# Encoder layer on one core: the first MLP product by Strassen's scheme, all hidden activations made first

## The chip, the core and the metric

The kernel runs on one core of a Trainium2 chip. The metric is the device time of one execution, in microseconds (us); lower is better. TensorE (PE) multiplies matrices, with its weight loads (PEld) listed apart; VectorE (DVE), ScalarE (ACT) and GpSimd (POOL) do elementwise work; SyncE (SP) and ScalarE issue the transfers (DMA) from and to DRAM. Matmul results land in PSUM banks; everything else lies in SBUF.

## What is computed

One encoder layer on 768 tokens (512 of a prompt, 256 of a sample), float32, width 1024. Mixer and cross attention come first; the change is in the MLP at the end:

```python
def _layer(x, ...):
    ...
    x = x + _rms_norm(_cross_attention(h, mem, xa_wq, xa_wkv, xa_wo, mem_g), g_post_xa)
    h = _rms_norm(x, g_pre_mlp)
    x = x + _rms_norm(jnp.square(jax.nn.relu(h @ w1)) @ w2, g_post_mlp)   # w1: 1024 x 4096, w2: 4096 x 1024
    return x
```

## The kernel before

**Three matmuls for one.** Every float32 operand is cut into a high part, rounded by a copy on ACT, and a low part, the rest, by a subtraction on DVE. A product is then three matmuls: high by high, high by low, low by high (`mm3`, L188 to L190; L1195 to L1197 in `up`). Activations are cut by `split` (L183 on ACT, L184 on DVE); weights by the class `Weights` (L108 on ACT, L109 on DVE), in units of 128x1024 elements. `W.get(key, ahead)` returns a unit and first emits the cutting of `ahead` further units in the order of the plan (`plan_c`). The high and low tiles of the units lie in groups of three in two slots; a slot comes free when all three units of its group have been used.

**Order.** The kernel is written in the Tile framework: the program order gives priorities, and the framework lays out each engine's queue before the run, by its own estimate of when operands and buffers are ready. On the chip each queue then runs in that order.

**The MLP.** The hidden width of 4096 is cut into eight blocks of 512. `up` makes one quarter (128 hidden features) of a block per weight unit: 8 steps of depth, three matmuls each, for the sample (256 columns) and for the prompt (512 columns), so 48 matmuls for a unit. ACT then applies relu (L1199) and POOL squares (L1200). `down` multiplies the block by its rows of `w2` by Strassen's scheme: the block's output, 768 tokens by 1024, is a 2x2 matrix product of halves of 384 tokens, 256 hidden features and 512 outputs, done with seven products instead of eight. A product is 18 matmuls of 512 columns (three groups of six). The sums and differences that the scheme needs are made on POOL: four per block of activations (L1218, 128x768) and four per block of weight quadrants (L997, 128x1024, in `quadrants`). Results are added into 18 accumulators (`acc`, six sets of three tiles of 128x512) by DVE from PSUM (L1239; in block 0 the first touch of a set is a copy on ACT, L1237). That is 24 additions per block, since product 1 goes into two sets.

**Sequence.** `STRASSEN` (L25) sets the order by hand: the seven products of block b are interleaved with the four quarters of `up` for block b + 1. Block 0's `up` stands before (the sample's part in the tail of the attention, L265, the prompt's at L1206). Block 7 is not in the scheme: `down_last` does it plainly, with 144 matmuls, combines the accumulators on POOL (L1257) and finishes the tiles (`finish`).

**Buffers.** Two high and two low tiles hold the cut activations of a product (`hh`, `hl`, `bufs=2`), and PSUM has four banks `mm` (for `up`) and four `y` (for `down`).

Of the kernel before, what the change touches and what calls it, by code (L numbers as in the profile page):

```python
# [6 lines left out]
F32 = mybir.dt.float32  # L7
F32R = mybir.dt.float32r
AF = mybir.ActivationFunctionType
ALU = mybir.AluOpType  # L10
# [14 lines left out]
STRASSEN = (("p", 1), ("up", 0), ("p", 2), ("p", 6), ("up", 1), ("p", 7), ("up", 2), ("p", 4), ("p", 5), ("up", 3), ("p", 3))  # L25
# [56 lines left out]
class Weights:  # L82
# [3 lines left out]
    def __init__(self, nc, new, raw, lo):  # L86
        self.nc, self.new, self.raw = nc, new, raw
        self.sub = lambda key: lo(key).tensor_tensor
        self.q, self.done, self.n = [], {}, 0
# [4 lines left out]
    def emit(self, upto):  # L94
        while self.n < min(upto, len(self.q)):
# [21 lines left out]
class Kernel:  # L117
# [75 lines left out]
    def run(self):  # L193
# [55 lines left out]
        self.hT = {}  # L249

        def h_tiles(s0, nt, side):
            pool, g = self.open(f"hx{s0}", side=side)
            self.hT[s0] = tuple(pool.tile([P, 8, nt * P], F32R, name=f"hx{s0}{n}") for n in "hl")
            return g

        g_h4 = h_tiles(*SEQS[1], "right")
# [3 lines left out]
        g_h0 = h_tiles(*SEQS[0], "left")  # L260
# [3 lines left out]
        first = self.hidden(up)  # L264
        self.up(0, 4, first, "up", 0)  # L265
# [3 lines left out]
        wp, g_w = self.open("wD", side="right")  # L269
        self.W.raw, self.w2pool = (wp, 1024, 2), wp  # L270
        pool, g = self.open("mlp", side="left")
        self.mlp(pool, up, first)
        for x in (g, g_up, g_h0, g_w, g_h4, g_ps, g_big, g_dram, g_const):
            self.close(x)
# [61 lines left out]
    def scratch(self):  # L336
# [7 lines left out]
        self.d_x1 = d.tile([NT, P, D], F32, name="d_x1")  # L344
        self.d_x2 = d.tile([NT, P, D], F32, name="d_x2")
# [614 lines left out]
    def plan_c(self):  # L960
# [14 lines left out]
        p1 = lambda b, m: w.plan(("w1", b, m), w1[:, :, b * 512 + m * P:b * 512 + (m + 1) * P], 8, P)  # L975

        for m in range(4):
            p1(0, m)
        for b in range(7):
            quad = dict(self.quadrants(w2[:, 4 * b:4 * b + 4]))  # L980
            for x, i in STRASSEN:
                if x == "up":
                    p1(b + 1, i)
                else:
                    w.plan(("w2", b, i), quad[i], 2, 512)
# [4 lines left out]
    def quadrants(self, w2):  # L990
# [3 lines left out]
        new = lambda: self.w2pool.tile([P, 2, 512], F32, tag="quad", bufs=5, name="quad")  # L994
# [5 lines left out]
        def p1():  # L1000
            for i in range(2):
                for j in range(2):
                    B[i, j] = new()
                    nc.sync.dma_start(B[i, j], w2[:, 2 * i:2 * i + 2, 512 * j:512 * j + 512])
# [176 lines left out]
    def hidden(self, pool):  # L1181

# [140 lines left out]
```

## Time and profile before

| | |
|---|---|
| median of 3 runs | 1213.06 us (1211.43 to 1223.36) |
| the profiled execution's own time | 1215.08 us |
| its span in the trace | 1213.3 us, 17783 instructions |
| mean granted TensorE clock over the span | 0.963 of full speed |
| PE busy | 1120.0 us (92%), 6800 matmuls |
| DVE busy | 708.1 us (58%) |
| ACT busy | 529.4 us (44%) |
| POOL busy | 355.5 us (29%) |

How to read it: the span is the trace's first to last instruction; the 1.8 us that the execution's own time has beyond it lie around it. Busy shares are means over the layer's stages. The MLP fills the span from about 713 us on, so shares of the MLP alone are read from windows of the trace. A busy PE is not a PE at its peak, so its pace is read from the starts of successive matmuls.

### The profile page before, as it was taken

Reading aid. Unit: us, or ns where it says so; the run is one execution under the profiler, and the core shown is the slowest. Engines: PE = TensorE matmul, PEld = TensorE weight load, DVE = VectorE, ACT = ScalarE, POOL = GpSimd, SP = SyncE. Lnnn points to the kernel's source line nnn. Section 1 sums busy time; section 2 is a strip of 40 time slices with the busy share of each in tenths; the row PEclk is TensorE's granted clock in tenths of the full one; section 3 lists DMA queues with packets and bytes.
Section 4 is the critical chain, followed back from the end, with each engine's and each line's share of the span. In section 5 each row is a group of like instructions: output and inputs, shape, how many; then the busy total and the mean of one; then the engine's idle time right before and its main releaser. Section 6 shows DMA issues by size and latency. Waiting matters only on the chain.

```text
span 1213.3 us, 17783 instructions
## 1 busy us (share of the span) xinstructions
PE 1120.0 (92%) x6800; PEld 958.7 (79%) x6800; DVE 708.1 (58%) x1263; ACT 529.4 (44%) x1119; POOL 355.5 (29%) x415
## 2 busy tenths in 40 slices
PE   6998999976959998899899989999999999999995
PEld 5887888865857887678787778888888888888884
DVE  5313455799789452455535646365658565658656
ACT  5336767755474333433434534443233332333322
POOL 5353210011111020011100136353536353526461
PEclk9999999988989698899899999999999999999998
DMA  6355311211312028732622233122212222212114
GB/s 199 98 180 160 94 53 37 78 35 36 75 48 92 28 93 253 239 122 82 231 70 70 88 122 96 43 75 65 88 53 76 63 70 70 87 52 61 44 57 169
DMA packets 108703, 113.81 MB, mean 94 GB/s; under 512 B 10079, under 2 KB 81867, under 8 KB 108619
## 3 DMA queue, kind: packets, MB, share of 16 engines
q1 hardware_dynamic: 100971, 99.55, 27.3%
q10 hardware_dynamic: 7648, 13.13, 2.9%
q8 instruction: 53, 0.87, 0.3%
q14 instruction: 31, 0.25, 0.1%
HBM read 91.27 MB, written 21.39 MB: 93 GB/s over the span
## 4 chain that ended last, share of the span: by engine, by line
PE 42%; issue 3%; POOL 2%; DVE 2%; DMA 1%; ACT 1%; POOLq 0%; DVEq 0%; ACTq 0%
PE up L1195 7%; PE up L1196 7%; PE up L1197 7%; PE y L189 5%; PE y L188 5%; PE y L190 5%; POOL y L1257 1%; DMA raw<-in_xa_wo 1%; PE xa L1156 1%; PE xa L1137 1%; PE mm L1121 1%; PE mm L1120 1%; PE mm L1119 1%; POOL rs L153 1%; PE mm L188 0%
## 5 line engine op out<-in xcount | busy, mean ns | idle before, releaser
L1200 POOL TENSOR_TENSOR hid<-hid 128x256 f32<-128x256 f32 (+1 forms) x64 | 61.1, 955 | 220.3 <-ACT hid L1199 220.3
L190 PE MATMUL y<-w,hl 128*128 128x512 f32 x318 | 123.8, 389 | 0.5 <-DVE hl L184 0.5
L189 PE MATMUL y<-w,hh 128*128 128x512 f32 x318 | 123.7, 389 | 0.0
L188 PE MATMUL y<-w,hh 128*128 128x512 f32 x318 | 123.7, 389 | 0.0
L1239 DVE TENSOR_TENSOR y<-y,y 128x512 f32<-128x512 f32 x72 | 48.9, 683 | 106.8 <-PE y L190 106.8
L1199 ACT ACTIVATE hid<-up 128x256 f32<-128x256 f32 (+1 forms) x64 | 31.2, 488 | 174.3 <-PE up L1197 174.3
L1195 PE MATMUL up<-hx0h,w 128*128 128x512 f32 x256 | 100.0, 390 | 1.0 <-DVE hx0l L184 1.0
L1196 PE MATMUL up<-hx0l,w 128*128 128x512 f32 x256 | 99.9, 390 | 0.0
L1197 PE MATMUL up<-hx0h,w 128*128 128x512 f32 x256 | 99.6, 389 | 0.0
L109 DVE TENSOR_TENSOR w<-raw,w 128x1024 fp32r<-128x1024 f32 (+1 forms) x58 | 78.8, 1365 | 31.4 <-ACT w L108 31.4
L997 POOL TENSOR_TENSOR quad<-quad 128x1024 f32<-128x1024 f32 x28 | 77.7, 2774 | 33.8 <-DVE w L109 20.2
L109 DVE TENSOR_TENSOR w<-quad,w 128x1024 fp32r<-128x1024 f32 x49 | 73.2, 1505 | 11.9 <-ACT w L108 11.9
L1195 PE MATMUL up<-hx4h,w 128*128 128x256 f32 x256 | 72.2, 282 | 4.2 <-ACT hid L1199 4.2
L1196 PE MATMUL up<-hx4l,w 128*128 128x256 f32 x256 | 71.7, 280 | 0.1
L1197 PE MATMUL up<-hx4h,w 128*128 128x256 f32 x256 | 71.4, 279 | 0.0
L108 ACT ACTIVATE w<-raw 128x1024 fp32r<-128x1024 f32 (+1 forms) x58 | 55.3, 963 | 35.7 <-DMA raw<-in_w_out 11.0
L190 PEld LDWEIGHTS y<-w,hl 128*128 128x128 f32 x318 | 59.7, 188 | 13.3 <-DVE hl L184 0.9
L189 PEld LDWEIGHTS y<-w,hh 128*128 128x128 f32 x318 | 59.7, 188 | 12.4
L188 PEld LDWEIGHTS y<-w,hh 128*128 128x128 f32 x318 | 59.7, 188 | 12.4
L183 ACT ACTIVATE hh<-hid 128x768 fp32r<-128x768 f32 x37 | 31.4, 848 | 83.2 <-PE y L189 64.0
L184 DVE TENSOR_TENSOR hl<-hid,hh 128x768 fp32r<-128x768 f32 x37 | 43.0, 1162 | 24.8 <-ACT hh L183 24.6
L1195 PEld LDWEIGHTS up<-hx0h,w 128*128 128x128 f32 x256 | 48.1, 188 | 10.4 <-DVE hx0l L184 1.2
(373 smaller groups left out, 3114.5 us busy)
## 6 DMA issues: line engine op xcount, KB each, us to landing
raw<-in_mlp_w SPq DMA_DIRECT2D x36, 512.0 KB, 4.5
quad<-in_mlp_w SPq DMA_DIRECT2D x28, 512.0 KB, 4.6
raw<-in_w_in SPq DMA_DIRECT2D x44, 256.0 KB, 3.0
d_x<-x ACTq DMA_DIRECT2D x12, 512.0 KB, 2.6
x<-d_x SPq DMA_DIRECT2D x12, 512.0 KB, 3.7
x<-in_x_prompt SPq DMA_DIRECT2D x8, 512.0 KB, 4.0
raw<-in_xa_wkv SPq DMA_DIRECT2D x16, 256.0 KB, 3.2
d_att<-parts SPq DMA_DIRECT2D x12, 256.0 KB, 2.0
```

Source lines behind the costliest of these rows:

```text
L108: self.nc.scalar.activation(hi[:, c], raw, AF.Copy)
L109: self.sub(key)(out=lo[:, c], in0=raw, in1=hi[:, c].bitcast(F32), op=ALU.subtract)
L184: nc.vector.tensor_tensor(out=lo, in0=src, in1=hi.bitcast(F32), op=ALU.subtract)
L188: nc.tensor.matmul(ps, lh, rh, start=first, stop=False)
L189: nc.tensor.matmul(ps, lh, rl, start=False, stop=False)
L190: nc.tensor.matmul(ps, ll, rh, start=False, stop=last)
L997: nc.gpsimd.tensor_tensor(out=out, in0=x, in1=y, op=ALU.subtract)
L1195: nc.tensor.matmul(ps, wh[:, k], hh[:, k], start=k == 0, stop=False)
L1196: nc.tensor.matmul(ps, wh[:, k], hl[:, k], start=False, stop=False)
L1197: nc.tensor.matmul(ps, wl[:, k], hh[:, k], start=False, stop=k == 7)
L1200: nc.gpsimd.tensor_tensor(out=r, in0=r, in1=r, op=ALU.mult)
L1239: nc.vector.tensor_tensor(out=y, in0=y, in1=ps, op=ALU.add)
```

## The change

Blocks 1 to 7 of the first product are done by Strassen's scheme too, and the two products of the MLP no longer alternate.

- **Sums of the activations.** `first_layer` makes the four sums of halves of the normed activations that the scheme needs (S1 to S4, each a high and a low tile of 128x4x384) once, in three column pieces, on DVE, POOL and ACT, before the prompt's part of block 0.
- **First layer.** For each of the blocks 1 to 7, seven products (`up`): a product is two quarters, each 4 steps of depth by three matmuls of 384 columns, so 24 matmuls. The results are combined from PSUM on DVE (and one copy per quarter on ACT) in the one hidden tile R, ACT does relu and square, and ACT's queue writes the quadrant to a new DRAM tensor `d_r`. R has one buffer.
- **Weight quadrants of w1.** `quadrants` now serves both products: four differences on POOL for each block of `w1` as well.
- **Second layer.** The hidden blocks are read back from `d_r`. `down` takes block 0 alone and then the pairs (1, 2), (3, 4), (5, 6): for each Strassen product both blocks' matmuls accumulate in the same PSUM group of twelve, so the additions into `acc` come once per pair. The cut activations have three buffers instead of two; quadrants of odd blocks have a pool of their own. PSUM groups use `mm` and `y` in turn.
- **Limits.** `W.limit` keeps the cutting of units from running ahead into a stage whose pool is not open yet.
- Squaring of blocks 1 to 7 moves from POOL to ACT.

```diff
-STRASSEN = (("p", 1), ("up", 0), ("p", 2), ("p", 6), ("up", 1), ("p", 7), ("up", 2), ("p", 4), ("p", 5), ("up", 3), ("p", 3))
+STRASSEN = (1, 2, 6, 7, 4, 5, 3)
+BLOCKS = ((0,), (1, 2), (3, 4), (5, 6))
...
-        first = self.hidden(up)
-        self.up(0, 4, first, "up", 0)
+        first = up.tile([P, 4, TOK], F32, tag="R", bufs=1, name="hid")
+        self.up_first(4, first, "up", 0)
...
+        self.W.limit = self.n_first + 7
+        pool, g = self.open("st", side="right")
+        self.first_layer(pool, up, first)
+        for x in (g, g_h):
+            self.close(x)
+        self.W.limit = None
+        pool, g = self.open("mlp", side="right")
+        self.w2more = pool
+        self.second_layer(pool, up, first)
...
+        for b in range(1, 8):
+            quad_b = q1(b)
+            for i in STRASSEN:
+                w.plan(("w1", b, i), quad_b[i], 4, 256)
+        self.n_first = len(w.q)
+        for bs in BLOCKS:
+            quad = [q2(b) for b in bs]
+            for i in STRASSEN:
+                for b, q in zip(bs, quad):
+                    w.plan(("w2", b, i), q[i], 2, 512)
...
+    def up(self, b, p, R, left, tags=("mm", "y"), ahead=3):
...
+        at = lambda j, i: R[:, 2 * j:2 * j + 2, 384 * i:384 * i + 384]
+        u, v, c = at(1, 0), at(1, 1), at(0, 1)
+        wh, wl = self.W.get(("w1", b, p), ahead)
+        for m in range(2):
+            ps = self.ps(tags[m], "up")[:, :384]
+            f = slice(m * P, (m + 1) * P)
+            for k in range(4):
+                nc.tensor.matmul(ps, wh[:, k, f], hh[:, k], start=k == 0, stop=False)
+                nc.tensor.matmul(ps, wh[:, k, f], hl[:, k], start=False, stop=False)
+                nc.tensor.matmul(ps, wl[:, k, f], hh[:, k], start=False, stop=k == 3)
+            if p == 1:
+                nc.scalar.activation(u[:, m], ps, AF.Copy)
+                continue
+            for out, x in {2: ((at(0, 0), u),), 6: ((u, u),), 7: ((v, u),), 4: ((c, v),), 5: ((v, v), (u, u)), 3: ((u, u),)}[p]:
+                nc.vector.tensor_tensor(out=out[:, m], in0=x[:, m], in1=ps, op=ALU.add)
+        done = {2: (0, 0), 4: (0, 1), 5: (1, 1), 3: (1, 0)}
+        if p in done:
...
+            nc.scalar.activation(r, r, AF.Relu)
+            nc.scalar.activation(r, r, AF.Square)
+            nc.scalar.dma_start(self.d_r[b][:, 2 * j:2 * j + 2, 384 * i:384 * i + 384], r)
...
+    def first_layer(self, pool, up, first):
...
+        for j in range(3):
...
+            op(V, s1, a21h, a22h, add)
+            op(G, t, a21l, a22l, add)
+            op(V, s1, s1, t, add)
+            op(V, s2, s1, a11h, sub)
+            op(V, s2, s2, a11l, sub)
+            self.split(s2, *(x[:, :, c] for x in S[2]))
+            op(G, t3, a11l, a21l, sub)
+            op(V, s3, a11h, a21h, sub)
+            op(V, s3, s3, t3, add)
+            self.split(s3, *(x[:, :, c] for x in S[3]))
+            sums.append((s1, c))
+            op(G, s2, a12h, s2, sub)
+            op(V, s2, s2, a12l, add)
+            self.split(s2, *(x[:, :, c] for x in S[4]))
+        self.up_first(0, first, "mm")
+        for s1, c in sums:
+            self.split(s1, *(x[:, :, c] for x in S[1]))
+        for b in range(1, 8):
+            for p in STRASSEN:
...
+                    self.up(b, p, R, left[p])
+            R = hid() if b < 7 else None
+
+    def second_layer(self, pool, up, first):
...
+        Rs = {0: first, 1: load(1)}
+        for bs in BLOCKS:
+            self.down(bs, pool, [Rs.pop(b, None) or load(b) for b in bs], acc)
...
+        for p in STRASSEN:
+            to = {1: "cu", 2: "c", 6: "u"}.get(p, str(p))
+            ops = []
+            for b, x in zip(bs, lefts):
+                hi, lo = (pool.tile([P, 2, 384], F32R, tag="h" + y, bufs=3, name="h" + y) for y in "hl")
+                self.split(x[p], hi, lo)
+                ops.append((hi, lo, *self.W.get(("w2", b, p), 3)))
+                if p == 1:
+                    S1 = x[5] = pool.tile([P, 2, 384], F32, tag="S", bufs=2, name="S")
+                    a00, a10, a11 = x[1], x[7], x[4]
+                    op(S1, a10, a11, ALU.add)
+                    op(a10, a00, a10, ALU.subtract)
+                    op(a00, S1, a00, ALU.subtract)
+                elif p == 2:
+                    op(x[2], x[2], x[6], ALU.subtract)
             for i in range(3):
                 c = slice(i * P, (i + 1) * P)
-                ps = self.ps("y")
-                for k in range(2):
-                    self.mm3(ps, hi[:, k, c], lo[:, k, c], wh[:, k], wl[:, k], k == 0, k == 1)
+                ps = self.ps(("mm", "y")[i % 2], "y")
+                for j, (hi, lo, wh, wl) in enumerate(ops):
+                    for k in range(2):
+                        self.mm3(ps, hi[:, k, c], lo[:, k, c], wh[:, k], wl[:, k], j + k == 0, j == len(ops) - 1 and k == 1)
                 for x in to:
                     y = acc[x][i]
-                    if b == 0 and x not in seen:
+                    if bs[0] == 0 and x not in seen:
                         nc.scalar.activation(y, ps, AF.Copy)
                     else:
                         nc.vector.tensor_tensor(out=y, in0=y, in1=ps, op=ALU.add)
...
```

## Rows read from the trace of the kernel before

**Rows 1.** Page part 1: engine, busy us (share of span) x instructions.
```profile
PE 1120.0 (92%) x6800; PEld 958.7 (79%) x6800; DVE 708.1 (58%) x1263; ACT 529.4 (44%) x1119; POOL 355.5 (29%) x415
```

**Rows 2.** Windows: stretch, length, busy us (count) of each engine; PEclk, DMA share, GB/s.
```profile
713.00:735.00 22.00, 21.70 (x96) 17.97 (x97) 7.90 (x7) 7.38 (x10) 11.50 (x7) 1.00 0.56 168
735.00:1160.00 425.00, 425.00 (x2199) 364.85 (x2198) 262.06 (x274) 148.68 (x200) 193.95 (x115) 1.00 0.23 69
```

**Rows 3.** PE's waits from 713 to 1160 us: total us, times, longest.
```profile
PE up L1195 <- DVE hx0l L184: 1.0, 1, 1.0
```

**Rows 4.** Timeline of PE: start us, us; first and last matmul of three runs.
```profile
837.94 0.39 PE L188 MATMUL y<-w,hh 128*128 128x512 f32 x1
...
845.87 0.39 PE L190 MATMUL y<-w,hl 128*128 128x512 f32 x1
846.10 0.28 PE L1195 MATMUL up<-hx4h,w 128*128 128x256 f32 x1
...
848.78 0.28 PE L1197 MATMUL up<-hx4h,w 128*128 128x256 f32 x1
848.90 0.39 PE L1195 MATMUL up<-hx0h,w 128*128 128x512 f32 x1
...
854.14 0.39 PE L1197 MATMUL up<-hx0h,w 128*128 128x512 f32 x1
```

**Rows 5.** Groups by line and shape from 700 us on: xcount | busy us, mean ns.
```profile
L997 POOL TENSOR_TENSOR quad<-quad 128x1024 f32<-128x1024 f32 x28 | 77.7, 2774 | 33.8 <-DVE w L109 20.2 <-issue 7.5 <-DVE hl L184 5.3
L109 DVE TENSOR_TENSOR w<-quad,w 128x1024 fp32r<-128x1024 f32 x49 | 73.2, 1505 | 11.9 <-ACT w L108 11.9
L108 ACT ACTIVATE w<-quad 128x1024 fp32r<-128x1024 f32 x49 | 50.1, 1049 | 3.3 <-DMA quad<-in_mlp_w 3.3
L1239 DVE TENSOR_TENSOR y<-y,y 128x512 f32<-128x512 f32 x72 | 48.9, 683 | 106.8 <-PE y L190 106.8
L184 DVE TENSOR_TENSOR hl<-hid,hh 128x768 fp32r<-128x768 f32 x37 | 43.0, 1162 | 24.8 <-ACT hh L183 24.6
L183 ACT ACTIVATE hh<-hid 128x768 fp32r<-128x768 f32 x37 | 31.4, 848 | 83.2 <-PE y L189 64.0 <-POOL hid L1200 10.0 <-DVE y L1239 6.5
L1218 POOL TENSOR_TENSOR hid<-hid 128x768 f32<-128x768 f32 x7 | 17.8, 2546 | 0.0
L1292 DVE TENSOR_TENSOR yg<-y,gain 128x512 f32<-128x512 f32 x9 | 6.4, 706 | 0.3
```

**Rows 6.** Timeline of DVE, 916 to 931 us.
```profile
918.15 2.76 DVE L109 TENSOR_TENSOR w<-quad,w 128x1024 fp32r<-128x1024 f32 x1
920.84 0.68 DVE L1239 TENSOR_TENSOR y<-y,y 128x512 f32<-128x512 f32 x1
921.44 2.27 DVE L109 TENSOR_TENSOR w<-quad,w 128x1024 fp32r<-128x1024 f32 x1
...
929.37 0.94 DVE L184 TENSOR_TENSOR hl<-hid,hh 128x768 fp32r<-128x768 f32 x1
```

**Rows 7.** Timeline of POOL, the same stretch.
```profile
917.98 1.85 POOL L1218 TENSOR_TENSOR S<-hid 128x768 f32<-128x768 f32 x1
919.91 2.71 POOL L1218 TENSOR_TENSOR S<-S,hid 128x768 f32<-128x768 f32 x1
922.58 2.85 POOL L1218 TENSOR_TENSOR hid<-hid 128x768 f32<-128x768 f32 x1
925.39 2.40 POOL L997 TENSOR_TENSOR quad<-quad 128x1024 f32<-128x1024 f32 x1
```

**Rows 8.** Timeline of DVE, 900 to 913 us: a weight cut with POOL idle.
```profile
901.73 1.22 DVE L109 TENSOR_TENSOR w<-quad,w 128x1024 fp32r<-128x1024 f32 x1
```

**Rows 9.** Timeline of POOL near the end: a lone sum of 128x512.
```profile
1175.74 1.28 POOL L1257 TENSOR_TENSOR y<-y,yu 128x512 f32<-128x512 f32 x1
```

**Rows 10.** Page part 6 and the DMA view: queue, xcount, KB each, median us to landing.
```profile
quad<-in_mlp_w SPq DMA_DIRECT2D x28, 512.0 KB, 4.6
d_z<-z ACTq DMA_DIRECT2D x4, 384.0 KB, 2.7
```

More of the change, by code (lines that the diff above doesn't have):

```diff
@@ L248, in run @@
         g_ps = self.banks(mm=3, tr=2, xa=2, up=1)
[L249 to L256, printed above, removed]
+        pool, g_h = self.open("hx", side="right")
+        hx = self.hx = [pool.tile([P, 8, TOK], F32R, name="hx" + x) for x in "hl"]
+        self.hT = {4: [x[:, :, 0:256] for x in hx], 0: [x[:, :, 256:TOK] for x in hx]}
         wp, g_w = self.open("wC", side="right")
@@ L988, in plan_c, with quadrants @@
                 w.plan(("w2", 7, i, j), w2[:, 28 + 2 * i:30 + 2 * i, 512 * j:512 * j + 512], 2, 512)
-    def quadrants(self, w2):
+    def quadrants(self, part, b=0):
         nc = self.nc
         B = {}
-        new = lambda: self.w2pool.tile([P, 2, 512], F32, tag="quad", bufs=5, name="quad")
+        shape = [P, *part(0, 0).shape[1:]]
+        new = lambda: (self.w2more if b % 2 else self.w2pool).tile(shape, F32, tag="quad", bufs=5, name="quad")
         def diff(out, x, y):
@@ L1178, in cross_tile, with up_first @@
         self.transposed(h, hh, hl, c.start)
-    def hidden(self, pool):
-        return [pool.tile([P, 2, TOK], F32, tag="hid", bufs=2, name="hid") for _ in range(2)]
-    def up(self, b, s0, R, tag, ahead=3, ms=range(4)):
+    def up_first(self, s0, R, tag, ahead=3):
         nc = self.nc
@@ L1190, in up @@
         c0 = 0 if s0 else 256
-        for m in ms:
-            wh, wl = self.W.get(("w1", b, m), ahead)
+        for m in range(4):
+            wh, wl = self.W.get(("w1", 0, m), ahead)
             ps = self.ps(tag, "up")[:, :n]
@@ L1197, in up @@
                 nc.tensor.matmul(ps, wl[:, k], hh[:, k], start=False, stop=k == 7)
[L1198 removed]
+            r = R[:, m, c0:c0 + n]
             nc.scalar.activation(r, ps, AF.Relu)
             nc.gpsimd.tensor_tensor(out=r, in0=r, in1=r, op=ALU.mult)
[L1202 to L1211 removed]
@@ L1222, in down @@
         seen = set()
-        def product(p, left, *to):
-            hi, lo = (pool.tile([P, 2, 384], F32R, tag="h" + x, bufs=2, name="h" + x) for x in "hl")
-            self.split(left, hi, lo)
-            wh, wl = self.W.get(("w2", b, p), 3)
+        for p in STRASSEN:
[13 more added lines that the diff above has]
+                    op(x[2], x[2], x[6], ALU.subtract)
```

93 lines of the change are left out of this document (50 added, 43 removed).

## The prediction

> **What bounds the kernel now.** The first view is the page's busy times: PE is busy for 92% of the span, far ahead of DVE and ACT [rows 1]. Such a share is a mean over the whole layer, so the second view is the MLP alone by windows. From 735 to 1160 us PE is busy for all of the 425 us at full clock, DVE for 262 us (62%), ACT for 149 us, POOL for 194 us (46%), and the DMA engines for 23% [rows 2]. The third view, PE's waits, says the same from the other side: 1.0 us in the whole MLP up to 1160 us [rows 3]. So PE alone sets the time of this stage, and everything else is hidden behind it. What is to be seen next is PE's pace, and the starts in its timeline give it. 36 matmuls of 512 columns in `down` take 7.93 us over 35 steps, 0.2266 us each; 24 of 256 columns 2.68 us over 23 steps, 0.1165 us; 24 of 512 columns in `up` 5.24 over 23, 0.2278 us [rows 4]. A block of `up` is thus 96 x (0.1165 + 0.2278) = 33.05 us, a block of `down` 126 x 0.2266 = 28.55 us, together 61.6 us.
>
> **PE's saving.** A block of the new `up` has 7 products of 24 matmuls, 168, of 384 columns. No row shows 384 columns; midway between 256 and 512 columns is 0.1722 us. The bounds are 1.5 times the 256 column step (0.1748) and 0.75 times the 512 column step (0.1709). A block is 168 x 0.1722 = 28.93 us, 4.12 us less than before, and seven blocks give back 28.9 us (25.7 to 30.4 by the bounds). The number of matmuls in `down` stays.
>
> The Trainium skill, "TensorE: Matmul & The Clock Gate", section "Wait — 56ns, not 53.3ns?", has starts N / 2.4 GHz plus about 2.5 ns apart, as an estimate 162.5 ns for 384 columns and a saving of 27.3 us instead of 28.9. The row for 512 columns has 226.6 ns where the rule has 215.8, so the rows are used.
>
> **First layer: does anything else become the bound?** For a block of 28.9 us DVE has 7 weight cuts at 1.5 us and 14 additions of 384 columns, each below the 0.68 us of 512 columns: 20 us. ACT has 7 weight copies (1.05), eight passes of 768 elements for relu and square (0.85) and two copies (below 0.85): 16 us. POOL has four differences at 2.8 us: 11 us [rows 5]. All fit, so I cost them at nothing. R has one buffer: block b + 1's first copy on ACT waits until block b's last quadrant is added (0.68), passed twice (1.7) and written (2.7 for 384 KB, rows 10 hold the nearest transfer), 5.1 us after PE's last matmul; behind that copy ACT's weight copies queue [rows 5, 10]. PE meanwhile writes into eight PSUM banks, four products or 16.5 us, and three more units are cut ahead. Without that cover it would be 6 x 5.1 = 31 us; I take 0.
>
> **Second layer: the shared port.** Here the cover shrinks. A pair is 252 matmuls, 57.1 us. For it DVE cuts 14 weight units and 14 activations and makes 24 additions; POOL makes 8 differences of 1024 elements and 8 of 768. Before, `up` stood between, with PE work that needs no activation cuts.
>
> The timelines show what DVE and POOL do to each other. A weight cut alone takes 1.22 us [rows 8], an activation cut 0.94 [rows 6], a POOL sum 1.85 or 2.40 [rows 7]. At 918.15 DVE starts a cut while POOL has a sum until 919.83; the cut ends at 920.91, 1.08 us after that. POOL's next sum, issued at 919.91, ends 1.71 us after the cut. DVE's next cut, issued at 921.44, ends at 923.71, 1.09 us after that sum, and so on [rows 6, 7]. They take turns: neither proceeds while the other holds the operands, and one group of POOL's sums that take 1.85 alone averages 2.55 over the stage [rows 5 to 7]. Additions from PSUM stay at 0.68 us throughout [rows 6].
>
> So cuts and sums add up. By the held times (1.08; 0.94 and 2.40 less the same 0.14 overhead; 1.71) a pair needs 14 x 1.08 + 14 x 0.80 + 8 x 2.26 + 8 x 1.71 = 58.1 us, 1.0 more than PE's 57.1. By the lone durations it needs 14 x 1.22 + 14 x 0.94 + 8 x 2.40 + 8 x 1.85 = 64.2 us, 7.1 more. A block before needed only 11 x 1.08 + 7 x 0.80 + 4 x 2.26 + 4 x 1.71 = 33.4 us (plus squares) of 61.6. The ceiling is set by bunching: POOL's work clusters around a pair's start, since products 6 and 7 want its results, and each of 16 sums there lets only one cut through. That is 34.0 + 16 x 0.94 = 49.0 us for 16 of the 28 cuts, and 12/28 of 57.1 for the rest: 73.5 us, 16.4 more. I take 5.5 us per pair, nearer the lone sum than the held one because the work is not spread evenly, and less than the lone sum because additions can wait in spare PSUM banks and one activation is cut ahead. Three pairs: 16.5 us (3 to 49).
>
> The Trainium skill, "SBUF — State Buffer", section "Who interferes with whom", calls this an exclusive lock held for a whole instruction, also by a DVE instruction with two SBUF inputs. With whole lone instructions that is 7.1 us per pair, 21.3 instead of 16.5, and the sum below would end at 1213.5. By that rule the trace agrees on the turns; the held times are shorter than the instructions.
>
> **The start.** The sums S1 to S4 are 33 DVE instructions of 512 elements (0.706 each, 23.3 us) and 9 on POOL (1.28 each, 11.5 us) [rows 5, 9]. Their cover is the prompt's part of block 0, 96 x 0.2278 = 21.9 us, and products 1 and 2, which need none of them, 8.3 us: 30.2 us until product 6 wants S2. DVE was busy for only 7.9 us from 713 to 735 [rows 2]. But these turns add up too: 34.8, three weight cuts (3.7) and three quadrant differences (7.2) make 45.7 us; S4 and the cuts of S1, some 10 us of it, are due only later. That leaves 5.5 us uncovered, less what starts before 713 us. I take 4 (0 to 15.5). Without the cover it would be 35.
>
> **Stage switch and transfers.** Block 0's first activation cut (0.85 on ACT, 1.16 on DVE) may have to wait for the last matmuls of the first layer, whose operands lie where the new pool opens: 2 us (0 to 6) [rows 5]. A pair reads 4 MB of quadrants and 3 MB of hidden activations on SP's queue; at the 168 GB/s that the window from 713 us shows that is 42 us of 57 [rows 2], so 0; if each 512 KB took its 4.6 us alone, 64 us, 7 per pair [rows 10]. `down_last` and the end stay as they are.
>
> **Sum.** Against the profiled execution: 1215.1 - 28.9 + 16.5 + 4 + 2 = 1208.7 us. The median of the runs shown lies 2.0 us below that execution, so I name 1208.
>
> **Rivals.** (a) The turns are hidden: pairs cost 1.0 to 4 us each, start and switch 3 to 4 in all, 1192 to 1202, for which 1195 stands. For it: DVE's additions per block are halved, and PE waited 1.0 us before. Against it: a port that is asked for 58.1 of every 57.1 us cannot be hidden.
>
> (b) The turns bind: every POOL sum in a pair holds up one cut, W and activation cuts come late for products 1, 2 and 6, and a pair costs 16.4 us more. 1215.1 - 28.9 + 49 + 6 = 1241 us, slower than before. It decides from about 12 us per pair on. For it: four cuts are due in every 8.2 us of PE, and while POOL is busy only about 2.7 get through (2.1 + 0.94 us each). Against it: POOL needs only 34 of 57 us, and sums whose operands are there early can run in the calmer products 4, 5 and 3. The section of the Trainium skill named above is the rule behind this rival.
>
> (c) The saving is not there: if 384 columns started at the step of 512, a block of `up` would take 38.3 us, and the end would be near 1274. The step for 256 columns speaks against it.
>
> **Chances.** Forecast 0.50 (its own range 1202 to 1222), (a) 0.30, (b) 0.18, (c) 0.02. About 1% is what a measurement of this kernel can tell from no change. Faster by over 1%: all of (a) and 0.04 of the forecast, 0.34. Slower: (b), (c) and 0.02 of the forecast, 0.22. Within 1%: 0.44. The range from 1191 to 1232 us leaves out the best packed part of (a), some 0.06, and the upper part of (b) with (c), some 0.13.
>
> **What the profile after would show.** PE's starts 0.172 us apart in the new `up`, and 28.9 us from a block's first matmul to the next one's: the saving is right. PE's waits at the first product 6 of block 1, on DVE's cut of S2: the start. PE's waits in the pairs, named as DVE cuts (`hl` or `w`), at about 5 us per pair and mostly at products 1, 2 and 6; DVE's mean for a weight cut well over 1.5 us; POOL busy for over 70% of a pair: the turns. No waits there and DVE's means unchanged would show (a), pairs of 70 us and more (b). Wrong altogether it would be if PE's waits named DMA of `d_r` or quadrants, or if ACT's wait for R reached PE.

## The result, and the profile after

The changed kernel takes 1251.84 us (median; 1249.33 to 1253.56) beside 1214.32 us of the kernel before: 1.029 times as long, 95% interval 1.0236 to 1.0352. The forecast was 1208 us, with a range from 1191 to 1232. The profiled execution took 1253.56 us, its span 1251.8 us, at a mean granted clock of 0.949.

Part 1 of the page after, as in [rows 1]: PE has 168 matmuls less and the same busy time in a span 38.5 us longer; DVE and POOL gained 110 and 50 us.

```profile
PE 1120.4 (90%) x6632; PEld 969.6 (77%) x6632; DVE 818.1 (65%) x1343; ACT 583.4 (47%) x1166; POOL 406.0 (32%) x396
```

The windows view after, for the two stages that were one in [rows 2]: the first layer (blocks 1 to 7), and the three pairs. Columns as there.

```profile
742.70:950.40 207.70, 207.70 (x1177) 207.59 (x1175) 136.68 (x157) 103.79 (x127) 78.81 (x32) 1.00 0.37 121
988.50:1205.80 217.30, 187.87 (x757) 148.00 (x756) 181.79 (x157) 76.78 (x87) 125.20 (x50) 0.93 0.23 79
```

In the first layer PE is busy without a gap. In the pairs it stands still for 29.4 of 217.3 us and its granted clock falls to 0.93. PE's waits of after from 690 to 1252 us name what is late; before, from 690 us on, no single one was over 1.3 us, and the MLP had the 1.0 us of [rows 3]:

```profile
PE y L191 <- DVE hl L185: 32.6, 11, 8.1
PE tp L179 <- DVE h L1059: 5.5, 1, 5.5
PE y L189 <- ACT hh L184: 5.0, 1, 5.0
PE up L1200 <- DVE hxl L185: 4.1, 1, 4.1
PE up L1200 <- ACT hid L1204: 1.3, 2, 0.8
```

The first is the activation cut in the pairs (and once in block 7), the third the switch between the stages, the second and fourth the start. From the starts of PE's timelines, before and after, the 38.5 us split like this (after less before, us):

| part | measured | predicted |
|---|---|---|
| start: prompt's part begins 718.65, was 713.30; and takes 24.06, was 21.9 | +7.5 | +4 |
| first layer of blocks 1 to 7: 207.75, `up` was 7 x 33.05 | -23.6 | -28.9 |
| switch (5.1) and block 0 of `down` (32.96, was 28.55) | +9.5 | +2 |
| pairs: 75.23, 75.79, 66.28, each 57.1 at the old step | +46.0 | +16.5 |
| block 7 (37.4, was 33.45) and the end (8.55, was 13.3) | -0.8 | 0 |
| sum | +38.6 | -6.4 |

The start is larger than its row. In the profiled execution of after, the attention ran 3.0 us ahead of before's: one matmul in its tail, `mm<-w,ol`, which waits 0.4 us for DVE in both, starts at 693.11 and at 696.07 us. Counted from that matmul, the prompt's part begins after 25.5 us in the changed kernel and after 17.2 before, so the start costs 8.3 + 2.2 = 10.5 us.

**What a late cut looks like.** The start of the first pair, in the timelines of DVE and then POOL (start us, us, line, count):

```profile
977.91 9.02 DVE L110 TENSOR_TENSOR w<-quad,w 128x1024 fp32r<-128x1024 f32 x3
986.86 9.28 DVE L185 TENSOR_TENSOR hl<-hid,hh 128x768 fp32r<-128x768 f32 x3
996.06 6.20 DVE L110 TENSOR_TENSOR w<-quad,w 128x1024 fp32r<-128x1024 f32 x2
...
1006.70 3.09 DVE L185 TENSOR_TENSOR hl<-hid,hh 128x768 fp32r<-128x768 f32 x1
```

```profile
982.47 15.93 POOL L1006 TENSOR_TENSOR quad<-quad 128x1024 f32<-128x1024 f32 x5
998.35 5.58 POOL L1305 TENSOR_TENSOR hid<-S,hid 128x768 f32<-128x768 f32 x2
```

Eight cuts in 24.3 us, 3.0 us each, whether they are of 1024 or of 768 elements (1.22 and 0.94 us alone, [rows 6, 8]); POOL's five sums take 3.2 us each (2.40 alone, [rows 7]). It is one cut, one sum, one cut, for as long as POOL has a sum ready. The cut at 1006.70 is the second block's activation for product 2, and PE has waited for it since 1001.8; between the rows shown, four additions (2.4 us) and one more weight cut (2.2 us) stand ahead of it in DVE's queue. PE's timeline when it comes:

```profile
1001.40 0.40 PE L190 MATMUL y<-w,hh 128*128 128x512 f32 x1
1009.85 0.80 PE L191 MATMUL y<-w,hl 128*128 128x512 f32 x1 [8.05 <-DVE hl L185]
1010.44 0.63 PE L189 MATMUL y<-w,hh 128*128 128x512 f32 x1
...
1015.56 0.44 PE L189 MATMUL y<-w,hh 128*128 128x512 f32 x1
```

After the wait the matmuls start 0.43 us apart instead of 0.23. The granted clock of that stretch is 0.50 of full speed, the lower of PE's two levels (1.2 GHz), and it is back at the higher one (2.4 GHz) 5.7 us later. This wait thus costs a third more than its length: 8.05 us of standing, and some 2.7 us of slow matmuls (13 steps in 5.71 us instead of 3.03). The pairs have three more such waits (6.9, 5.2 and 4.6 us, each with the granted clock at 0.50 behind it) and two of 1.4 us, behind which it stayed at 1.00. The windows of the slow stretch and of 20 us around it, and one that has no long wait:

```profile
1009.85:1015.50 5.65, 5.65 (x13) 4.46 (x14) 3.32 (x4) 0.00 (x0) 1.82 (x1) 0.50 0.30 96
1000.00:1020.00 20.00, 11.95 (x40) 9.21 (x39) 15.26 (x14) 3.13 (x4) 10.80 (x5) 0.74 0.17 53
1100.00:1120.00 20.00, 20.00 (x87) 16.03 (x86) 14.04 (x15) 8.96 (x10) 7.12 (x3) 1.00 0.23 74
```

Over all pairs (988 to 1205 us), the groups by line and shape that answer to [rows 5]:

```profile
L110 DVE TENSOR_TENSOR w<-quad,w 128x1024 fp32r<-128x1024 f32 x39 | 74.1, 1936 | 0.0
L1006 POOL TENSOR_TENSOR quad<-quad 128x1024 f32<-128x1024 f32 x21 | 65.4, 3135 | 31.8 <-DMA quad<-in_mlp_w 26.6 <-DVE w L110 4.9
L185 DVE TENSOR_TENSOR hl<-hid,hh 128x768 fp32r<-128x768 f32 x37 | 57.7, 1569 | 12.6 <-ACT hh L184 12.6
L1337 DVE TENSOR_TENSOR y<-y,y 128x512 f32<-128x512 f32 x35 | 23.8, 679 | 11.0 <-PE y L191 10.9
```

A weight cut went from 1505 to 1936 ns, an activation cut from 1162 to 1569, a quadrant sum from 2774 to 3135. The additions from PSUM stayed at 679 ns. POOL's second number matters too: of its 31.8 us idle before quadrant sums, 26.6 wait for the quadrants' transfers, so these set when a run of sums begins.

### The profile page after: what moved, and what is told of

Read it like the earlier page. It is cut to its first block, busy times and chain, and to the rows that moved or that the text cites. A ratio compares the mean times of both kernels' runs of the same rounds, so it can differ in the third digit from the quotient of the medians.

```text
span 1251.8 us, 17757 instructions
## 1 busy us (share of the span) xinstructions
PE 1120.4 (90%) x6632; PEld 969.6 (77%) x6632; DVE 818.1 (65%) x1343; ACT 583.4 (47%) x1166; POOL 406.0 (32%) x396
## 4 chain that ended last, share of the span: by engine, by line
PE 33%; DVE 9%; issue 6%; POOL 3%; ACT 2%; DMA 1%; DVEq 0%; POOLq 0%; ACTq 0%
PE up L1224 5%; PE up L1225 5%; PE up L1223 5%; DVE w L110 4%; PE y L191 4%; PE y L189 3%; PE y L190 3%; DVE hl L185 2%; POOL y L1345 1%; DMA raw<-in_xa_wo 1%; PE up L1200 1%; PE xa L1165 1%; PE up L1201 1%; PE up L1202 1%; PE xa L1146 1%
## 5 line engine op out<-in xcount | busy, mean ns | idle before, releaser
L1006 POOL TENSOR_TENSOR quad<-quad 128x1024 f32<-128x1024 f32 x56 | 156.8, 2808 | 153.4 <-DMA quad<-in_mlp_w 82.5
L110 DVE TENSOR_TENSOR w<-quad,w 128x1024 fp32r<-128x1024 f32 x98 | 179.3, 1849 | 20.5 <-ACT w L109 20.5
L109 ACT ACTIVATE w<-quad 128x1024 fp32r<-128x1024 f32 x98 | 99.7, 1050 | 47.1 <-PE up L1225 32.9
L1230 DVE TENSOR_TENSOR hid<-hid,up 128x384 f32<-128x384 f32 x98 | 51.1, 547 | 49.4 <-PE up L1225 28.3
L1223 PE MATMUL up<-hxh,w 128*128 128x384 f32 x224 | 75.8, 339 | 0.0
L1225 PE MATMUL up<-hxh,w 128*128 128x384 f32 x224 | 75.8, 339 | 0.0
L1224 PE MATMUL up<-hxl,w 128*128 128x384 f32 x224 | 75.8, 339 | 0.0
L109 ACT ACTIVATE whi<-raw 128x512 fp32r<-128x512 f32 (+1 forms) x61 | 37.6, 622 | 31.7 <-DMA raw<-in_w_in 8.6
L560 DVE SCALAR_TENSOR_TENSOR y<-stage,cw,y 128x770 f32<-128x770 f32 x48 | 49.7, 1036 | 2.3 <-ACT y L558 1.8
L110 DVE TENSOR_TENSOR w<-raw,w 128x1024 fp32r<-128x1024 f32 (+1 forms) x30 | 31.6, 1061 | 27.4 <-ACT w L109 27.4
L190 PE MATMUL att<-wlo,hh 128*128 128x256 f32 x144 | 42.3, 294 | 1.6 <-POOL wlo L110 1.3
```

The lines of the kernel that those rows point to most:

```text
L109: self.nc.scalar.activation(hi[:, c], raw, AF.Copy)
L110: self.sub(key)(out=lo[:, c], in0=raw, in1=hi[:, c].bitcast(F32), op=ALU.subtract)
L190: nc.tensor.matmul(ps, lh, rl, start=False, stop=False)
L560: nc.vector.scalar_tensor_tensor(out=y, in0=xp[:, j:j + 770], scalar=tap(j), in1=y, op0=ALU.mult, op1=ALU.add)
L1006: nc.gpsimd.tensor_tensor(out=out, in0=x, in1=y, op=ALU.subtract)
L1223: nc.tensor.matmul(ps, wh[:, k, f], hh[:, k], start=k == 0, stop=False)
```

## The experiments

The theory in question, **turns**: cuts on DVE and sums on POOL, each reading two operands from SBUF, proceed one at a time, and the cuts are late for that. Its rival, **lateness**: POOL is slow and its sums are late for the products that want them. Where a single execution is shown, segments are compared and not only totals, since the attention ahead of the MLP varies: with the same code up to there, the prompt's part began at 716.1 us in one experiment and at 722.9 in another, in both 25.5 us after the matmul named above.

**POOL keeps its hours, but reads nothing** (`e1_writes`). The numbers of the second layer are meaningless here; the work of PE, DVE and ACT is all there.

```diff
         def diff(out, x, y):
+            if second:
+                nc.gpsimd.tensor_tensor(out=out[:, :, 0:4], in0=x[:, :, 0:4], in1=y[:, :, 0:4], op=ALU.subtract)
+                for _ in range(3):
+                    nc.gpsimd.memset(out[:, :, 4:], 0.01)
+                return out
```
(and the same for the activations' sums)

> In the second layer each sum on POOL is cut to four columns per half (so that it still waits for the same operands), and the rest of its tile is filled with three POOL writes of a constant, which read nothing; the second layer's numbers are thus meaningless. POOL is kept about as long per sum. Turns theory (DVE's cuts and POOL's sums hold each other up because both read two operands): with nothing read on POOL the cuts fall back to 1.22 and 0.95 us, pairs of 75.2, 75.8 and 66.3 us fall to 57 to 61, the time to 1203 to 1212 us. Lateness theory (POOL's row of sums before product 6 is simply too long): POOL's row stays, pairs stay at 68 to 76 us, the time over 1240.

1208.32 us, 1211.67 for the kernel before beside it. The pairs, 984.0 to 1160.4 us, by windows and by groups:

```profile
984.00:1160.40 176.40, 176.40 (x757) 142.13 (x756) 133.50 (x155) 76.58 (x87) 120.91 (x162) 1.00 0.29 98
```

```profile
L1009 POOL MEMSET quad<- 128x1016 f32 x56 | 52.1, 947 | 17.2 <-DVE w L110 11.6 <-DVE hl L185 3.2 <-DMA quad<-in_mlp_w 2.0
L110 DVE TENSOR_TENSOR w<-quad,w 128x1024 fp32r<-128x1024 f32 x39 | 47.1, 1247 | 0.7 <-ACT w L109 0.7
```

POOL is busy for 121 us of the pairs, nearly as long as in the changed kernel (125), and PE has no wait at all: 58.80 us for each pair, at full clock. A weight cut is back at 1247 ns, though the writing fills go on beside it. So it is not that POOL is busy; it is that POOL reads. The Trainium skill, "SBUF — State Buffer", section "Who interferes with whom", says that a DVE instruction with two SBUF inputs contends with a GpSimd instruction that reads SBUF and not with one that only writes it; the 1247 ns agree. Compared with this run, the pairs' 40.9 us more in the changed kernel are 29.4 us of standing and 11.5 us of slow matmuls (PE's busy time, 187.87 less 176.40).

The run shows a second thing. With nothing lost to turns the whole change gains 3.4 us, one execution against one, which is within what single executions of one kernel differ by (before: 1211.43 to 1223.36). Start, switch, block 0 and PE's own steps take back nearly all of the saving.

**The same with a third of the fills** (`e2_one_write`).

```diff
-                for _ in range(3):
+                for _ in range(1):
```

> As the kernel with three writes per sum, but with one write, so that POOL's row in the second layer is less than half as long (the second layer's numbers are meaningless here too). Turns theory: no difference to three writes, pairs 57 to 60 us. Lateness theory: only here do the pairs fall, to 57 to 60 us. If pairs stay over 65 us in both, POOL has nothing to do with it and DVE's own 46.6 us per pair or its order is the cause.

1208.94 us, pairs of 58.80 us each, with POOL busy for 57 us of the three pairs instead of 121. How long POOL writes makes no difference; together with `e1_writes`, where POOL kept its hours and the pairs fell all the same, the lateness theory falls.

**All sums of the second layer on DVE** (`e3_dve_sums`): nothing left out.

```diff
-            nc.gpsimd.tensor_tensor(out=out, in0=x, in1=y, op=ALU.subtract)
+            (nc.vector if second else nc.gpsimd).tensor_tensor(out=out, in0=x, in1=y, op=ALU.subtract)
...
-        op = lambda out, x, y, op: nc.gpsimd.tensor_tensor(out=out, in0=x, in1=y, op=op)
+        op = lambda out, x, y, op: nc.vector.tensor_tensor(out=out, in0=x, in1=y, op=op)
```

> The 16 sums of a pair are made on DVE, none on POOL; nothing is left out. Turns theory: no turns are left, cuts are back at 1.22 and 0.95 us, but DVE's own work rises from 46.6 to 46.6 + 8 x 1.22 + 8 x 0.94 = 63.9 us, so all pairs take 64 to 68 us, about 1225 to 1232 us in all. Lateness theory: the sums take half as long, products 6 wait less, pairs 58 to 62 us. If DVE's work alone were the cause, pairs would grow beyond 76 us.

1221.3 us in one execution, 30 us less than the changed kernel. The pairs take 59.5, 62.2 and 61.8 us. Both times are below what the turns theory gave (64 to 68, 1225 to 1232), and the pairs alone would fit the other theory's 58 to 62; it is the two runs above that decide. The 63.9 us was too high as a sum of single durations: DVE's instructions in the pairs add up to 188 us, but it is busy for 174.6, since each starts some 0.07 us before the last one ends (as in [rows 6], 918.15 + 2.76 against 920.84). Giving DVE more work made DVE faster at its old work, as its groups from 990 to 1180 us show:

```profile
L110 DVE TENSOR_TENSOR w<-quad,w 128x1024 fp32r<-128x1024 f32 x39 | 47.7, 1246 | 0.1
L185 DVE TENSOR_TENSOR hl<-hid,hh 128x768 fp32r<-128x768 f32 x36 | 37.4, 1044 | 2.9 <-ACT hh L184 2.8
L1006 DVE TENSOR_TENSOR quad<-quad 128x1024 f32<-128x1024 f32 x21 | 25.5, 1216 | 0.0
```

A quadrant sum takes 1216 ns there, two fifths of its 3135 ns on POOL, and holds up no cut for longer than that.

**The start** (`e4_start`): the loads of block 1's `w1` quadrants wait until the tail of the attention has written its last column, so that POOL's differences of them cannot stand between the tail's steps.

```diff
                     B[i, j] = new()
+                    if hold:
+                        nc.scalar.activation(B[i, j][:, 0, 0:1], self.hx[1][:, 7, TOK - 1:TOK].bitcast(F32), AF.Copy)
                     nc.sync.dma_start(B[i, j], part(i, j))
```

> The loads of the four w1 quadrants of block 1 wait for the last cut of the attention's tail, so POOL's differences can't stand in front of the tail's norm steps on POOL. If that order is what delays the start, PE's wait for DVE h at the last transposes falls from 5.5 to 1 to 2 us, the wait for hxl from 4.1 to 1 to 3, and the time by 4 to 8 us (1246 to 1250), as long as product 6 of block 1 does not wait. Rival: the sums S1 to S4 hold DVE at that point, then only the first wait falls and the second stays at 4 us or a new wait of that size appears at product 1, 2 or 6 of block 1.

1252.22 us: no gain in the total. PE's waits, beside those of after above:

```profile
PE y L191 <- DVE hl L185: 33.5, 11, 8.1
PE y L189 <- ACT hh L184: 10.3, 1, 10.3
PE up L1227 <- DVE w L110: 7.0, 1, 7.0
PE up L1202 <- DVE hxl L185: 1.6, 1, 1.6
PE tp L179 <- DVE h L1061: 1.3, 1, 1.3
```

The two waits of the start fell from 9.6 to 2.9 us and the prompt's part began at 709.3 us instead of 718.7, but block 1 then waited 7.0 us for its first weight cut, and the switch grew to 10.3. The expected 4 to 8 us did not come, and the new wait is the sign that the expectation gave for its rival. That the differences held up the tail is shown (the prompt's part begins 17.8 us after the attention's matmul named above, instead of 25.5); that their removal from there is worth anything is not: the work only moved. The timelines of POOL and then DVE in the changed kernel have the place:

```profile
707.66 0.19 POOL L153 TENSOR_SCALAR rs<-ss 128x1 f32<-128x1 f32 x1
707.93 2.34 POOL L1006 TENSOR_TENSOR quad<-quad 128x1024 f32<-128x1024 f32 x1
710.22 0.55 POOL L154 TENSOR_TENSOR rs<-rs,mhalf 128x1 f32<-128x1 f32 x1
```

```profile
712.36 3.38 DVE L110 TENSOR_TENSOR w<-quad,w 128x1024 fp32r<-128x1024 f32 x1
715.65 1.75 DVE L1252 TENSOR_TENSOR s<-hxh 128x512 f32<-128x512 f32 x1
717.32 1.28 DVE L185 TENSOR_TENSOR hxl<-tp,hxh 128x512 fp32r<-128x512 f32 x2
```

On POOL, two steps of a norm that PE's last transposes wait for, 0.19 and 0.55 us, with a weight difference of 2.34 us in between. On DVE, the cut that the prompt's part waits for (717.32) stands behind a weight cut of the new stage and a first sum for S1.

**Moving the activations' sums into the first layer** (`g1_operands`), where POOL is busy for 79 of 207.7 us: made on POOL there, seven operands per block written to DRAM and read back one by one.

```diff
+    def operands(self, b, p, a00, a10, a01, a11):
+        if p == 5:
+            op(s1, a10, a11, ALU.add)
+            store(5, s1)
+            op(s2, s1, a00, ALU.subtract)
+            store(2, s2)
+            op(a10, a00, a10, ALU.subtract)
+            store(3, a10)
+        else:
+            op(a01, a01, self.s12[1], ALU.subtract)
+            store(6, a01)
```

> The sums of the activations are made on POOL in the first layer, as soon as a block's quadrants are there, and all seven operands of a block are written to DRAM; the second layer only loads, cuts and multiplies them. Its weight sums stay on POOL (8 per pair). Nothing is left out. Turns theory: a pair has 14 x 1.08 + 14 x 0.80 + 8 x 2.26 = 44 us for cuts and sums in turn, and DVE 46.6 us plus at most 8 waits of 1 to 2 us: pairs fall from 75.2, 75.8 and 66.3 to 59 to 64 us, the time to about 1218 to 1228 us; the first layer stays at 29 to 30 us per block. If the activations' sums had no part in it, pairs stay over 70 us.

1261.86 us (the kernel before took 1218.44 beside this run and the next two, each of one execution), worse. The pairs did fall, to 65.7, 71.8 and 61.1 us, two of them not as far as expected. But the first layer took 227.8 us instead of 203.8 to 207.8, and the switch 13.8:

```profile
PE y L191 <- DVE hl L185: 16.1, 10, 5.2
PE y L189 <- ACT hh L184: 13.6, 1, 13.6
PE up L1223 <- ACT w L109: 9.9, 2, 5.3
...
```

The waits name ACT, whose queue now also issues seven writes per block behind POOL's sums, in order with the weight copies. Which of these it was that held the copies up is open; the operands' way through DRAM was not tried on another queue.

**And the two sums t1 and t2 of each block of `w2` on DVE** (`g2_mixed`).

```diff
-            nc.gpsimd.tensor_tensor(out=out, in0=x, in1=y, op=ALU.subtract)
+            (nc.vector if v and second else nc.gpsimd).tensor_tensor(out=out, in0=x, in1=y, op=ALU.subtract)
...
-            B["t1"] = diff(B[0, 1], B[0, 1], B[0, 0])
-            B["t2"] = diff(new(), B[1, 1], B["t1"])
+            B["t1"] = diff(B[0, 1], B[0, 1], B[0, 0], True)
+            B["t2"] = diff(new(), B[1, 1], B["t1"], True)
```

> As the kernel with seven operands per block, and two of the four weight sums per block (t1 and t2, the chain in front of product 6) are made on DVE. Turns theory: DVE's own work is 46.6 + 4 x 1.22 = 51.5 us, four waits for POOL remain: pairs of 58.8 (the pace of a pair without waits) to 61 us, 3 to 8 us less in all than with all weight sums on POOL. If DVE's own work is what binds, pairs are no shorter than there.

1249.98 us. Pairs 61.3, 63.8, 61.1; first layer 227.2 and switch 14.7 as before it. The three are 12.3 us shorter together than with all weight sums on POOL, more than the 3 to 8 expected, though none is within the expected 61: the first two got shorter, as the turns have it, the third did not.

**And the start, and accumulators placed at first use** (`g3_all`): the two right-hand quadrants of block 1 held as in `e4_start`, S2 of all three pieces made first.

```diff
+                    if hold and j:
+                        nc.scalar.activation(B[i, j][:, 0, 0:1], self.hx[1][:, 7, TOK - 1:TOK].bitcast(F32), AF.Copy)
...
-        acc = {x: [pool.tile([P, 512], F32, name=f"y{x}{i}") for i in range(3)] for x in "cu7453"}
+        acc = {}
...
+                    if (x, i) not in acc:
+                        acc[x, i] = pool.tile([P, 512], F32, name=f"y{x}{i}")
```

> As the kernel with mixed weight sums, with three changes of order: the quadrants that the first POOL differences need are loaded only after the attention's last cut (the others, which products 1 and 2 need, at once); of S1 to S4 the sums S2 of all three pieces come first; the accumulators are allocated at their first use, so that the first cut activations of the second layer lie where the normed activations lay and not under the last product's operand. Expected: the prompt's part of block 0 starts about 9 us earlier, as in the kernel with held loads, without its 7.0 us wait at product 1 (2 us at most at products 1, 2 and 6); the gap before block 0 of the second layer falls from 5 to 10 us to 2 or less; together 10 to 16 us less than the kernel with mixed weight sums alone. If the start's wait only moves to product 6, 3 to 6 us are gained there.

1248.53 us. The prompt's part began at 710.5 us; a wait of 6.4 us for a weight cut stands in block 1, and the switch is 16.9 us. A miss: most of the gain expected did not come.

**Back to `e3_dve_sums`: an early place for block 0's cuts** (`h1_early_cuts`).

```diff
+        scratch, g_scratch = self.open("sum", side="right")
-        new = lambda tag: pool.tile([P, 4, P], F32, ...)
+        new = lambda tag: scratch.tile([P, 4, P], F32, ...)
...
+        self.close(g_scratch)
+        self.hp, self.g_hp = self.open("h", side="left")
...
-                hi, lo = (pool.tile([P, 2, 384], F32R, tag="h" + y, bufs=3, name="h" + y) for y in "hl")
+                hi, lo = (self.hp.tile([P, 2, 384], F32R, tag="h" + y, bufs=3, name="h" + y) for y in "hl")
```

> All sums of the second layer on DVE, as in e3_dve_sums, and one more edit: the cut activations of the second layer get a pool of their own, opened over the scratch of the S sums, which is free soon after the start of the first layer, and not over the operands of the last products. If the gap at the stage switch (7.1 us in e3_dve_sums, a wait for ACT hh) comes from the place of those tiles, the cuts of block 0 are made during the last product of the first layer, the gap falls to about 1 us, and the time is 6 us below e3_dve_sums, about 1215 us. If it comes from ACT's queue, where the cut stands behind the last relu and square, which wait for PE's last matmul, the gap stays at 5 to 7 us and so does the time, about 1221 us.

1214.89 us, 1.001 of the kernel before (0.9989 to 1.0031), as expected. The gap at the switch is gone: the second layer's first matmul starts 0.18 us after the first layer's last. Half of its worth came back 8 us later as a wait of 4.5 us, also for `hh`: product 6 of block 0 wants S2, whose sums now queue on DVE between additions. Switch and block 0 together went from 39.3 to 35.7 us. The pairs are those of `e3_dve_sums` (59.1, 62.3, 62.6), and their window says what bounds them:

```profile
985.20:1168.90 183.70, 178.72 (x756) 142.01 (x755) 175.08 (x197) 76.86 (x87) 15.19 (x9) 0.98 0.27 93
```

DVE is busy for 175 of 183.7 us. PE meanwhile had a shorter step here than in `e3_dve_sums`, 0.2267 us for 512 columns instead of 0.2333 (21 steps between these rows), which is 1.7 us less per pair, and the pairs got no shorter for it:

```profile
1010.88 0.39 PE L190 MATMUL y<-w,hh 128*128 128x512 f32 x1
...
1015.64 0.39 PE L190 MATMUL y<-w,hh 128*128 128x512 f32 x1
```

So with all sums on DVE it is DVE that bounds the pairs, closely followed by PE.

**Six of a pair's sixteen sums back on POOL** (`h2_six_on_pool`): those due latest, to relieve DVE.

```diff
-            B["t3"] = diff(new(), B[1, 1], B[0, 1])
+            B["t3"] = diff(new(), B[1, 1], B[0, 1], False)
...
-                    op(a10, a00, a10, ALU.subtract)
+                    nc.gpsimd.tensor_tensor(out=a10, in0=a00, in1=a10, op=ALU.subtract)
...
-                    op(x[2], x[2], x[6], ALU.subtract)
+                    nc.gpsimd.tensor_tensor(out=x[2], in0=x[2], in1=x[6], op=ALU.subtract)
```

> h1_early_cuts, and six of the sixteen sums of a pair back on POOL: in each block the weight difference for product 7, the activation difference for product 7 and the one for product 3, all of them due late. By the turns theory the sum of what DVE must do counts, and what POOL holds of its port: DVE's own work in a pair was 14 x 1.25 + 14 x 1.04 + 24 x 0.68 + 8 x 1.22 + 8 x 0.95 = 65.7 us, and loses 2 x 1.22 + 4 x 0.95 = 6.2; POOL's six take 2 x 2.26 + 4 x 1.71 = 11.4 us of the port, which the additions from PSUM (16.4 us) do not need. Pairs then fall from 60.6 to 66.2 us to about 59 to 62, some 8 us for the three. If any sum on POOL costs DVE its whole length, the pairs get 5 us longer each instead, about 15 us more than h1_early_cuts.

1230.24 us, 15.4 us more than `h1_early_cuts`; 1.0148 of before (1.0121 to 1.0174). The pairs take 71.0, 68.6 and 58.9 us, 14.5 more in all. This is the total that the worse of the two expectations gave, though not 5 us each: the third pair got shorter. The pairs by windows, PE's waits in them, and one of POOL's sums:

```profile
986.80:1185.50 198.70, 182.28 (x758) 146.23 (x757) 179.70 (x184) 76.72 (x87) 57.41 (x24) 0.96 0.25 87
```

```profile
PE y L191 <- DVE hl L185: 15.1, 9, 4.6
PE y L190 <- DVE w L110: 1.3, 1, 1.3
```

```profile
L1328 POOL TENSOR_TENSOR hid<-hid 128x768 f32<-128x768 f32 x6 | 18.2, 3036 | 30.0 <-DVE hl L185 30.0
```

Six sums per pair were moved off DVE and left it no less busy (179.7 us, 175.1 in `h1_early_cuts`), because instructions that stayed grew by the waiting (a weight cut from 1246 to 1412 ns, a quadrant sum on DVE from 1217 to 1399). POOL is busy for only 57 of 198.7 us and still costs 15.

**The start once more** (`h3_held` on `h2_six_on_pool`, `h4_best` on `h1_early_cuts`): only the right-hand quadrants of block 1 held, by the first two lines of the diff of `g3_all`.

> h2_six_on_pool, and the loads of the two right-hand quadrants of block 1 of w1 held until the attention's tail has written its last column, so that POOL's differences of block 1 do not stand between the tail's steps. If these sums delay the start of the prompt's part (718.7 us in the changed kernel, 709.3 in e4_start), it begins by 712 us, and the time falls by 5 us or more against h2_six_on_pool. If the S sums must be made in any case and only the place of the wait moves, as in e4_start, a wait of 4 to 7 us appears at block 1's first products and the time stays within 2 us of h2_six_on_pool.

> h1_early_cuts with the held right-hand quadrants of block 1 (all sums of the second layer on DVE). h3_held against h2_six_on_pool had the prompt's part begin 10.6 us earlier, and then lost 3.2 us at block 1's fourth product (DVE w) and some of the rest later; its profiled execution was 5.8 us shorter, its median 0.9 us longer. If the 5.8 us are real, this version is at about 1209 us, 5 us (0.4%) below the kernel before; if only the place of the wait moves, it is at 1215 us, as h1_early_cuts and as the kernel before.

1231.1 us (1.0154 of before, 1.0112 to 1.0195) and 1214.11 us (0.9989, 0.9965 to 1.0014): no difference from the versions without it. In `h4_best` the prompt's part began at 714.5 instead of 721.3 us, but block 1 waited 2.8 us for a weight cut, ran with a granted clock of 0.50 for 6 us after it, and the first layer took 213.6 instead of 203.8 us. Of these 9.8 us, 5.8 are block 1's, and 3.9 a longer step of PE in the other blocks that has no known cause (see below). In neither place tried was the work of the start free. `h4_best` has the lowest median of the complete versions, and it is no faster than the kernel before by what the measurement can tell.

Not tried: the new first layer in the old alternating order, quadrants loaded earlier so that POOL's sums need not run back to back, and more buffers for cut activations.

## Why the prediction was wrong

**What bounds.** Right for before: PE alone, and its pace read from starts. Wrong in what followed from it: the changed kernel's pairs are bound by DVE and POOL together, not by PE.

**PE's saving** was 23.6 instead of 28.9 us. The step for 384 columns was taken as 0.1722 us. The changed kernel's starts have it at 0.1767 (49 steps from the first to the last of these rows):

```profile
761.78 0.34 PE L1223 MATMUL up<-hxh,w 128*128 128x384 f32 x1
...
770.44 0.34 PE L1224 MATMUL up<-s4l,w 128*128 128x384 f32 x1
```

That is above the upper bound of 0.1748 and makes 29.7 us a block. Yet `e1_writes`, `e3_dve_sums` and `h1_early_cuts` ran the same stage in 203.85 us, a step of 0.1733, a saving of 27.5. Both steps occur within one execution too: in `g2_mixed` the first layer has 0.1733 from 744 us, 0.1767 from 771 and 0.1733 again from 800. Of the 5.3 us missed, 3.9 lie in that difference, whose cause is open, and 1.4 in the interpolation. (The lower bound of the saving, 25.7, is 25.8 by its own terms.)

**First layer, costed at nothing beyond PE**: right. No wait of PE stands between the first and the last matmul of the seven blocks, and the single buffer of R cost PE nothing.

**Second layer, the step that failed.** The mechanism was named; the price taken for it was wrong. The forecast took 5.5 us per pair, and 15.3 came: 46.0 for three, of which 29.4 us are PE standing still, 11.5 slow matmuls and 5.1 a longer step. So the turns alone made PE stand for 9.8 us per pair, nearly twice what was allowed for them, and what they brought with them was not in the sum.

The 5.5 us came from the sum of all work of a pair set against the pair's length, with spare PSUM banks and one activation cut ahead as the buffer. But POOL's sums run back to back as soon as their operands land, five quadrant sums in 15.93 us, and for that time DVE makes one cut in 3 us where PE wants one in about 2 (four in each 8.2 us, as rival (b) had it). PE's first long wait, 8.05 us, comes at product 2 of the first pair, so the buffer did not cover that. POOL was busy for 58% of the pairs, not over 70%.

The ceiling of 16.4 us per pair rests on sixteen turns in 49.0 us, 3.06 us each, and the timeline has 3.0. That a pair's 15.3 us come so near it is in part luck: the ceiling priced only turns, and these cost 9.8. (It also puts lone sums on POOL beside held cuts on DVE; with held times for both it would be 14.2.)

The two terms that were left out: the clock's fall after long waits, 11.5 us in the pairs, since the forecast priced waits by their length alone; and PE's step. For 512 columns it is 0.2333 us in the pairs of the changed kernel and not 0.2266 [rows 4], 1.7 us per pair, also where nothing waits (`e1_writes`: 252 x 0.2333 = 58.80). Rows of after, 39 steps apart:

```profile
1103.77 0.39 PE L190 MATMUL y<-w,hh 128*128 128x512 f32 x1
...
1112.87 0.39 PE L190 MATMUL y<-w,hh 128*128 128x512 f32 x1
```

**The start** was put at 4 us and cost 7.5 in the table, 10.5 when counted from the same matmul, within its bounds, but elsewhere than said. PE did not wait for S2 in block 1; it waited before the prompt's part (9.6 us, behind which slow matmuls cost another 1.7), because the first quadrant differences and weight cuts of the new stage came ahead of the tail's last steps in POOL's and DVE's queues. I had looked for the cover behind the start and not for the work that would move ahead of it.

**The switch** was put at 2 us (0 to 6) and cost 5.1, and block 0 another 4.4: 2.7 of that are slow matmuls behind the switch's wait, 0.8 the longer step, and its one wait beyond 0.3 us is of 0.7. `h1_early_cuts` confirms the cause of the gap: with tiles of their own the cuts come early and the gap goes.

**Transfers at nothing**: right for PE, none of whose waits names a DMA; POOL's sums did wait for the quadrants (26.6 us in the pairs).

**The rivals.** (b) came, by its mechanism; 1241 us was its time, 1251.84 the median, and the pairs' 46.0 us beside its 49 hold the terms named above that it did not have. The point from which it decides, 12 us per pair, was passed with these terms. Its chance of 0.18 was too low; what was said against it (POOL needs only 34 of 57 us) was a mean over a pair. (a) has its test in `e1_writes`, one execution: with the turns away the time was 1208 us and not 1195, since start, switch and steps cost 13 us more than (a) gave them. So even pairs at 5.5 us would not have brought 1208, but about 1220 (1208.3 and three times 5.5 less the 1.7 that are in it). (c) did not come.

## What to carry to other kernels

When two engines take turns, add up the turns inside the shortest stretch in which one of them has its work queued back to back, and compare it with the next deadline; a mean over the stage hides it. Here such work belonged on the faster of the two engines, even though that engine was the busier one. A version in which the suspect engine only writes tells in one run whether turns or lateness are the matter. Before saving matmuls on a PE that is 100% busy, find what fills the other engines beside it: here the saving took away the stage in which they could catch up, and the waits that came in its place took the saving back. In the pairs of the changed kernel the four long waits each cost more than their length, because PE's clock fell with them.

## What was unexpected of the hardware

- Without any wait and at full clock, PE's step had two values. For 384 columns they are 0.1733 and 0.1767 us, and the first layer can have both in one execution (`g2_mixed`). For 512 columns they are 0.2267 (the rows of before; `h1_early_cuts` to `h4_best`) and 0.2333 (the pairs of all other versions); between `e3_dve_sums` and `h1_early_cuts` the edit only changes where the cut activations and the scratch of the S sums lie. What makes the difference is open. A step read at one place is good to about 3%.
- POOL's fills of 128x1016 (947 ns) ran beside DVE's cuts at no cost to these (1247 ns), while POOL's sums of the same tiles, reading, more than doubled a cut to 3.0 us.
- Moving sums to a slower and less busy engine cost 15 us in `h2_six_on_pool`, with that engine busy for 29% of the pairs.
